# Hybrid decoder trunk on one core: first transfers issued from two queues in another sequence, transfer times in the planner changed, stage order redrawn

## The chip, the core and the metric

The kernel runs on 1 core of one Trainium2 chip. The metric is the device time of one execution in microseconds (us), lower is better: the median of 3 runs. Engines are named as the profile names them: PE (TensorE matmul), PEld (its weight loads), DVE (VectorE), ACT (ScalarE), POOL (GpSimd), SP (SyncE). SPq is the stream of instructions on SP that issues the transfers.

## The reference

Two residual layers over one sequence of 256 positions, width 1024, all float32. Each layer normalises x (RMSNorm), projects it with one wide matrix whose columns belong to several mixers, runs the mixers, multiplies each branch by a SiLU gate and adds the output projection to x.

```python
h = _rmsnorm(x, norm_g[layer])
proj = jnp.einsum('bsd,de->bse', h, w_in)
# layer 0: u_val u_gate z_a q_b k_b v_b z_b, each 512 columns
y_a = _conformer_conv(u_val, u_gate, ...) * silu(z_a)   # 31-tap causal convolution, LayerNorm, SiLU
y_b = moba_attention(q, k, v) * silu(z_b)               # 8 heads of 64
# layer 1: q_c, keys and values, gates, z_c, q_d, k_d, v_d, z_d
y_c = nsa_attention(...) * silu(z_c)   # compressed, selected and window branch
y_d = banded_attention(..., sinks) * silu(z_d)
x = x + jnp.einsum('bse,ed->bsd', concat(y), w_out[layer])
```

## The kernel before

The 256 positions are two token blocks of 128 partitions (`NB` = 2), the width is 8 chunks of 128 (`KC` = 8). A projection of 512 columns is one weight "name" (`ug`, `uv`, `qb`, `kb`, `vb`, `zb`, `za` in layer 0; `kv`, `cc`, `qc`, `kd`, `qd`, `zc`, `zd` in layer 1; `o00` to `o11` for the output projections). `load_w` (L486) loads it in four quarters of 512 KB, each into one of 5 `raw` buffers, and splits each quarter into two parts: `hi` (a cast, ACT or DVE) and `lo` = raw - hi (DVE or POOL). A product then takes three matmuls, hi*hi, hi*lo and lo*hi (`mm3`, L606). Only `ug` is multiplied unsplit, in plain float32, from `raw_ug` and the transposed input `h32`, so that it can begin before any norm is known; the factor of the norm is put in afterwards (`first_block`, L573, with `square_sum`, L560: squares of x, the power -1/2 on POOL, a matmul that spreads the factor `rb`, then `ht` = h32 * rb, its cast `hhi` and the rest `hlo`). The accumulators of projections are two PSUM banks (`pj`), those of attention scores two more (`s`).

In layer 0 the convolution (stages `conv 0` and `conv 1`) is 120 instructions on DVE that add one tap each into `acc_m` or `acc_o`, while PE goes on with qb, kb, vb, zb, za and the attention (`attb` j: scores and softmax of a pair of heads; `pvb` j: the product with the values). `ln`, `ln 2`, `o0` follow, then `norm1 0` and `norm1 1` (the norm of layer 1, one per token block, `norm_block`, L590), which need the output projections of their block: `o0 00` and `o0 01` for block 0, `o0 10` and `o0 11` for block 1.

**What sets the order.** No instruction is issued where it is written. `Recorder` (L172) collects all operations; `issue` (L256) then plays them through a model and emits every engine's instructions in the order that the model gives. Its loop takes for each engine the ready operation with the smallest key and issues the earliest of them (L326):

```python
k = (t, o.seq, 0, 0.0) if e == "SP" else (t, o.rank, o.piece, -o.level)
```

`t` is the modelled start; `rank` is the place of the operation's stage in the list `ORDER` (L404, 128 names), which decides between operations that could start at the same modelled time, that is, whenever an engine has a queue of ready work. Transfers go in program order (`seq`). On the chip each engine runs its instructions in the emitted order, whatever is ready. The costs are in `_cost` (L122): a transfer costs its queue 70 ns (L127). When data land is modelled in L359 to L364: a shared bus from 1400 ns after the issue, 360 bytes per ns, and 900 ns to the end. `free` (L267) says when each engine can begin.

**The first transfers** are all issued by SP in this sequence: `idn` (68 KB: identity and norm weights), `h32` chunk 0, the first half of `ug` quarter 0, chunk 1, the second half, chunks 2 and 3, `ug` quarter 1, x piece 0 and 1 (`X_AT`, L418; together token block 0), `h32` chunks 4 to 7, `ug` quarter 2, x piece 2 and 3 (token block 1), `ug` quarter 3, `prm`, `shp`, then `uv`.

All operations are recorded by one helper, so the profile gives line L384 for nearly all of them; they are told apart by tile names.

## Time and profile before

| | |
|---|---|
| runs | 273.28, 273.89, 274.37 us; median 273.89 |
| profiled execution | 273.76 us, of which its span (first to last instruction) is 271.8 us |
| PE | 262.1 us busy (96% of the span) |
| DVE, ACT, POOL | 195.8, 172.1, 113.8 us busy (72, 63, 42%) |
| granted TensorE clock, mean | 0.994 |
| transfers | 44.89 MB, 165 GB/s in the mean |

The profiled execution has 1.96 us outside its span and stands 0.13 us below the median. Busy PE is modelled: matmuls overlap, so the distance from one start to the next says more than a duration.

### The profile page before, as it was taken

How to read it: one execution, taken by the hardware profiler on the slowest of the kernel's cores; microseconds unless marked ns; L12 is line 12 of the kernel's file. 1: busy time of each engine (PE TensorE's matmuls, PEld its weight loads, DVE VectorE, ACT ScalarE, POOL GpSimd, SP SyncE). 2: the span in 40 equal slices, each digit the busy share in tenths (PEclk: the TensorE clock that was granted, in tenths of full speed). 3: DMA queues.
4: the chain of work that ended last, by engine and by line, in shares of the span. 5: the costliest groups of instructions: out<-in, count | busy, mean ns of one | idle time of the engine just before them, and what ended most of it. 6: DMA issues, size and time to landing. Idle time of an engine off the chain costs nothing.

```text
span 271.8 us, 5006 instructions
## 1 busy us (share of the span) xinstructions
PE 262.1 (96%) x1693; PEld 215.2 (79%) x1693; DVE 195.8 (72%) x510; ACT 172.1 (63%) x457; POOL 113.8 (42%) x145
## 2 busy tenths in 40 slices
PE   7998999999979999999999999999899999999995
PEld 4787987878859989888779888777689977778884
DVE  1379899999998995748977513398999765666241
ACT  2249579799745975836456503598897767886200
POOL 0000079989974504300323746149756042542000
PEclk9999999999979999999999999999999999999999
DMA  6998896655561290521675745699376400000013
GB/s 185 372 407 278 274 329 194 193 165 182 191 219 58 83 295 17 162 67 38 187 247 133 240 140 151 196 393 326 112 239 210 154 4 0 2 1 1 2 39 115
DMA packets 28361, 44.89 MB, mean 165 GB/s; under 512 B 3376, under 2 KB 10288, under 8 KB 28336
## 3 DMA queue, kind: packets, MB, share of 16 engines
q1 hardware_dynamic: 28336, 44.58, 50.3%
q8 instruction: 13, 0.21, 0.3%
q14 instruction: 12, 0.10, 0.1%
HBM read 43.26 MB, written 1.05 MB: 163 GB/s over the span
## 4 chain that ended last, share of the span: by engine, by line
PE 54%; DVE 29%; DMA 8%; issue 3%; SPq 2%; ACT 1%; POOL 0%; DVEq 0%
PE po L384 15%; DVE acc_m L384 8%; DVE acc_o L384 6%; PE pj_za L384 4%; PE pj_zd L384 4%; PE pj_qc L384 4%; PE pj_zc L384 3%; PE pj_zb L384 3%; PE po_c L384 3%; DMA raw_ug<-in_e_w_in_dram 2%; DMA raw_qd<-in_o_w_in_dram 2%; PE pj_cc L384 2%; PE pt_c L384 2%; PE pj_kv L384 2%; DVE ht L384 2%
## 5 line engine op out<-in xcount | busy, mean ns | idle before, releaser
L384 POOL TENSOR_SCALAR p_c<-p_c,r_c 128x128 f32<-128x128 f32 (+1 forms) x32 | 19.4, 621 | 22.8 <-DVE r_c L384 13.9
L384 DVE SCALAR_TENSOR_TENSOR acc_o<-hc,cw,acc_o 128x256 f32<-128x256 f32 x58 | 28.0, 482 | 0.2
L384 DVE SCALAR_TENSOR_TENSOR acc_m<-hc,cw,acc_m 128x256 f32<-128x256 f32 x58 | 27.9, 481 | 0.0
L384 PE MATMUL po<-hi_o,yh 128*128 128x512 f32 (+1 forms) x72 | 26.9, 378 | 0.0
L384 PE MATMUL po<-lo_o,yh 128*128 128x512 f32 (+1 forms) x72 | 26.5, 373 | 0.0
L384 PE MATMUL po<-hi_o,yl 128*128 128x512 f32 (+1 forms) x72 | 26.1, 370 | 0.0
L384 PE MATMUL pj_ug<-h,raw_ug 128*128 128x256 f32 x64 | 17.1, 424 | 1.2 <-DMA raw_ug<-in_e_w_in_dram 1.2
L384 ACT CAST hi_o<-raw_o 128x1024 fp32r<-128x1024 f32 x16 | 16.7, 1055 | 1.9 <-PE pj_zc L384 1.1
L384 DVE TENSOR_TENSOR lo_o<-raw_o,hi_o 128x1024 fp32r<-128x1024 f32 x13 | 15.7, 1221 | 2.5 <-PE pj_zd L384 1.7
L384 POOL TENSOR_TENSOR rsx<-ssx,mhalf 128x1 f32<-128x1 f32 x4 | 2.3, 569 | 34.5 <-DVE ssx L384 34.5
L384 PEld LDWEIGHTS pj_ug<-h,raw_ug 128*128 128x128 f32 x64 | 13.2, 214 | 4.4 <-issue 1.5
L384 ACT ACTIVATE p_c<-sn,mn_c 128x256 f32<-128x256 f32 (+1 forms) x32 | 14.3, 451 | 2.5 <-DVE mn_c L384 2.4
L384 PEld LDWEIGHTS po<-lo_o,yh 128*128 128x128 f32 x72 | 13.5, 188 | 2.5 <-issue 0.5
L384 PEld LDWEIGHTS po<-hi_o,yh 128*128 128x128 f32 x72 | 13.5, 189 | 2.3 <-issue 0.2
L384 PEld LDWEIGHTS po<-hi_o,yl 128*128 128x128 f32 x72 | 13.6, 189 | 2.1
L384 POOL TENSOR_TENSOR lo_kb<-raw_kb,hi_kb 128x1024 fp32r<-128x1024 f32 x3 | 7.3, 2452 | 18.4 <-ACT hi_kb L384 18.4
L384 DVE CUSTOM_DVE_ANT_0 sn<-s_c,shp 128x256 f32<-128x256 f32 (+1 forms) x32 | 10.7, 351 | 3.3 <-ACT p_c L384 3.3
L384 POOL TENSOR_SCALAR p_b<-p_b,r_b 128x128 f32<-128x128 f32 (+1 forms) x16 | 6.7, 436 | 12.6 <-DVE r_b L384 12.6
L384 POOL TENSOR_SCALAR p_d<-p_d,r_d 128x128 f32<-128x128 f32 (+1 forms) x16 | 6.7, 439 | 9.9 <-ACT p_d L384 3.3
L384 ACT ACTIVATE p_b<-sn,mn_b 128x256 f32<-128x256 f32 (+1 forms) x16 | 7.2, 450 | 4.9 <-DVE mn_b L384 4.7
L384 PE MATMUL pj_zc<-hhi,lo_zc 128*128 128x256 f32 x32 | 9.4, 294 | 0.7 <-DVE lo_zc L384 0.7
L384 PE MATMUL pj_zb<-hhi,hi_zb 128*128 128x256 f32 x32 | 9.9, 310 | 0.0
(332 smaller groups left out, 930.1 us busy)
## 6 DMA issues: line engine op xcount, KB each, us to landing
raw_o<-in_w_out_dram SPq DMA_DIRECT2D x16, 512.0 KB, 4.6
raw_uv<-in_e_w_in_dram SPq DMA_DIRECT2D x4, 512.0 KB, 7.7
raw_qb<-in_e_w_in_dram SPq DMA_DIRECT2D x4, 512.0 KB, 4.7
raw_kb<-in_e_w_in_dram SPq DMA_DIRECT2D x4, 512.0 KB, 5.5
raw_vb<-in_e_w_in_dram SPq DMA_DIRECT2D x4, 512.0 KB, 4.4
raw_zb<-in_e_w_in_dram SPq DMA_DIRECT2D x4, 512.0 KB, 3.5
raw_za<-in_e_w_in_dram SPq DMA_DIRECT2D x4, 512.0 KB, 4.2
raw_kv<-in_o_w_in_dram SPq DMA_DIRECT2D x4, 512.0 KB, 3.7
```

The source lines that it names most:

```text
L384: getattr(self.real[e], method)(*args, **kw)
```

## The change

Three things are changed, and no arithmetic.

1. The issue of three transfers (`idn` and the two halves of `ug` quarter 0) goes from SP to the queue of ACT, through `nc.first`: in the model these three cost SP nothing, and ACT is taken to be free from 3200 ns rather than 1880. The sequence of the rest changes: `h32` chunks 4 to 7 now come right after `ug` quarter 1, ahead of `ug` quarter 2, and all four pieces of x come after quarter 2, ahead of quarter 3.
2. The model's transfers: 440 ns on the queue instead of 70; landing begins 1300 ns after the issue, at 300 bytes per ns until 8500 ns and 410 after, and ends 750 ns later.
3. `ORDER` has the same 128 names in another order.

Places of some stages in `ORDER` (0 is the first to be served), before and after:

| stage | before | after | stage | before | after |
|---|---|---|---|---|---|
| conv 0 | 26 | 51 | o0 00 | 25 | 64 |
| conv 1 | 58 | 44 | o0 01 | 24 | 74 |
| attb 0 | 49 | 27 | o0 10 | 45 | 18 |
| attb 1 | 32 | 13 | o0 11 | 123 | 86 |
| attb 2 | 59 | 6 | norm1 0 | 20 | 50 |
| attb 3 | 81 | 114 | norm1 1 | 0 | 5 |
| w zc 0 | 30 | 19 | qd 1 | 14 | 66 |
| w zc 1 | 51 | 36 | qt d | 27 | 9 |
| sc 0 | 5 | 15 | cmp | 63 | 49 |

```diff
--- before.py
+++ after.py
@@ -108,7 +108,7 @@
 class Op:
     def __init__(self, alts, reads, writes):
         self.alts, self.reads, self.writes = alts, reads, writes
-        self.deps, self.succ = set(), []
+        self.deps, self.succ, self.queue = set(), [], None
 
 
 def _views(args, kw):
@@ -124,7 +124,7 @@
     n = w[0].size() if w else 512
     small = min(v.base.psum for v in r) if r else False
     if method == "dma_start":
-        return 70.0
+        return ISSUE_NS
     if engine == "PE":
         if method == "transpose":
             return 109.0
@@ -177,6 +177,7 @@
         self.real = dict(PE=nc.tensor, ACT=nc.scalar, DVE=nc.vector, POOL=nc.gpsimd, SP=nc.sync)
         for e, n in zip(self.ENGINES, ("tensor", "scalar", "vector", "gpsimd", "sync")):
             setattr(self, n, _Front(self, e))
+        self.first = _Front(self, "SP", "ACT")
 
     def stage(self, name):
         self.rank = ORDER.index(name)
@@ -264,7 +265,7 @@
             if o.alts[0][1] == "dma_start":
                 c += 3000
             o.level = c + 130 + max((s.level for s in o.succ), default=0.0)
-        free = dict(PE=600.0, ACT=1880.0, DVE=600.0, POOL=600.0, SP=280.0)
+        free = dict(FREE)
         work = {}
         bus, mode = 0.0, (P, P)
         port = dict(DVE=0.0, POOL=0.0)
@@ -360,8 +361,8 @@
                 o.on = "SP"
                 v = (o.writes or o.reads)[0]
                 bytes_ = 4 * v.size() * (v.box[0][1] - v.box[0][0])
-                bus = max(bus, t + 1400) + bytes_ / 360.0
-                o.end = bus + 900
+                bus = _landing(bus, t, bytes_)
+                o.end = bus + 750
             for b in o.banks:
                 b.last[e] = o.end
             o.done = True
@@ -376,7 +377,7 @@
                 if method == "together":
                     yield from (("PE", *a) for a in args)
                 else:
-                    yield e, method, args, kw
+                    yield o.queue or e, method, args, kw
 
         for e, method, args, kw in parts():
             args = [a.real() if isinstance(a, Ap) else a for a in args]
@@ -385,14 +386,30 @@
 
 
 class _Front:
-    def __init__(self, rec, engine):
-        self.rec, self.engine = rec, engine
+    def __init__(self, rec, engine, queue=None):
+        self.rec, self.engine, self.queue = rec, engine, queue
 
     def __getattr__(self, method):
-        return lambda *args, **kw: self.rec.record((self.engine, method, args, kw))
+        def f(*args, **kw):
+            op = self.rec.record((self.engine, method, args, kw))
+            if self.queue:
+
+                op.queue = self.queue
+                op.alts[0] = (*op.alts[0][:4], 0.0, *op.alts[0][5:])
+            return op
+        return f
+
+
+def _landing(bus, t, nbytes):
+
+    t = max(bus, t + 1300.0)
+    early = min(nbytes, max(0.0, SLOW_UNTIL - t) * 300.0)
+    return t + early / 300.0 + (nbytes - early) / 410.0
 
 
 CYCLE, WINDOW_NS = 5 / 12, 10240 / 3
+FREE = dict(PE=600.0, ACT=3200.0, DVE=600.0, POOL=600.0, SP=280.0)
+ISSUE_NS, SLOW_UNTIL = 440.0, 8500.0
 SWITCH = 95.0
 START = {(64, 128): 120.0, (128, 64): 65.0, (128, 32): 45.0}
 LATENCY = dict(PE=dict(PE=0.0, ACT=200.0, DVE=200.0, POOL=200.0, SP=200.0),
@@ -401,21 +418,20 @@
                POOL=dict(PE=135.0, ACT=100.0, DVE=60.0, POOL=96.0, SP=100.0),
                SP=dict(PE=250.0, ACT=100.0, DVE=100.0, POOL=100.0, SP=100.0))
 EXTRA = dict(copy=(0.0, 20000.0), minus=(80.8, 0.0), scale=(0.0, 20000.0, 20000.0))
-ORDER = ["norm1 1", "attd 2", "w ug 1", "norm0 g0", "pvc 11", "sc 0", "norm0 1", "pvb 3", "kv 1", "w qc 0",
-         "w cc 1", "attc 10", "w o10 1", "zd 2", "qd 1", "w ug 0", "pvd 1", "kd 1", "norm0 r1", "vb 0", "norm1 0",
-         "vb 1", "w qd 0", "zc 3", "o0 01", "o0 00", "conv 0", "qt d", "ln 2", "cc", "w zc 0", "w zb 0", "attb 1",
-         "w o00 0", "o1 10", "norm0 0", "w o01 1", "pvd 0", "pvc 31", "pvb 2", "w qc 1", "ug", "w uv 0", "attc 30",
-         "attc 11", "o0 10", "attd 0", "pvc 00", "attd 1", "attb 0", "zb 0", "w zc 1", "kv 0", "w o10 0", "zb 1",
-         "xc", "qt c", "qc 1", "conv 1", "attb 2", "zb 2", "sc 1", "pvc 21", "cmp", "zd 0", "pvb 0", "zc 0", "kd 0",
-         "pvc 01", "attc 21", "qc 0", "uv", "pvb 1", "zc 1", "qb 0", "zb 3", "qb 1", "zc 2", "o1 00", "pvc 10",
-         "za 0", "attb 3", "pvc 30", "o1 01", "norm0 r0", "w kb 1", "hid", "pvd 2", "w kd 1", "w o01 0", "qd 0",
-         "za 1", "w qb 0", "w kv 0", "w uv 1", "w qb 1", "pvc 20", "w za 1", "attd 3", "w qd 1", "w za 0", "w vb 0",
-         "ln", "w zd 1", "w vb 1", "zd 1", "w kv 1", "w cc 0", "attc 31", "zd 3", "attc 20", "kb 0", "attc 01",
-         "w o11 1", "kb 1", "w o11 0", "pvd 3", "w o00 1", "norm0 g1", "w zd 0", "attc 00", "w zb 1", "o1 11",
-         "o0 11", "za 2", "w kb 0", "za 3", "w kd 0"]
+ORDER = ["norm0 r1", "za 1", "norm0 g1", "w qb 1", "pvb 2", "norm1 1", "attb 2", "zb 1", "kv 1", "qt d", "norm0 1",
+         "attc 01", "norm0 0", "attb 1", "w kb 0", "sc 0", "za 0", "o1 01", "o0 10", "w zc 0", "za 3", "pvb 0",
+         "zd 1", "zc 2", "zc 3", "zb 2", "pvb 1", "attb 0", "uv", "w cc 1", "qb 0", "w o11 0", "w o00 0", "pvc 11",
+         "w kv 1", "za 2", "w zc 1", "zd 2", "w kd 1", "w ug 0", "attc 00", "attd 2", "w uv 1", "pvb 3", "conv 1",
+         "zc 0", "w ug 1", "qb 1", "zb 0", "cmp", "norm1 0", "conv 0", "zb 3", "pvc 01", "hid", "ln 2", "pvd 0",
+         "w o11 1", "w uv 0", "kd 0", "w qb 0", "w qd 1", "pvc 31", "pvc 00", "o0 00", "attc 20", "qd 1", "o1 00",
+         "pvd 1", "pvc 10", "attc 10", "sc 1", "w o10 1", "pvc 21", "o0 01", "w kb 1", "attc 31", "pvd 2", "qc 1",
+         "vb 0", "ug", "w zd 1", "w vb 0", "w zb 1", "w zb 0", "kb 0", "o0 11", "ln", "attc 30", "w za 0",
+         "w o01 1", "kv 0", "vb 1", "xc", "w qc 1", "kd 1", "pvc 20", "qt c", "zd 0", "w za 1", "w qd 0", "cc",
+         "norm0 g0", "w kd 0", "w o01 0", "w cc 0", "attd 1", "w zd 0", "pvd 3", "zd 3", "qc 0", "qd 0", "zc 1",
+         "pvc 30", "attb 3", "attc 21", "o1 10", "w kv 0", "w o10 0", "attd 3", "attc 11", "kb 1", "o1 11",
+         "w qc 0", "w o00 1", "norm0 r0", "w vb 1", "attd 0"]
 RAWS, PARTS = 5, 9
 WARM = 7
-X_AT = ((), (0, 1), (2, 3))
 SUMS_ON_ACT = ('qb', 'kb')
 HEADS_ON_ACT = ("qb", "kb")
 IN_TURN = ("raw", "hi", "lo", "pj", "qn8", "s")
@@ -442,7 +458,7 @@
     idn = const.tile([P, P + KC], F32, name="idn")
     ident, ng = idn[:, :P], idn[:, P:]
     prm = const.tile([P, NPRM], F32, name="prm")
-    nc.sync.dma_start(idn, i["idn"])
+    nc.first.dma_start(idn, i["idn"])
     pieces_x = [(b, slice(q * 512, (q + 1) * 512)) for b in range(NB) for q in range(2)]
 
     def load_x(n):
@@ -499,18 +515,18 @@
             else:
                 raw = raws.tile([P, 2, 512], F32, tag="raw", bufs=RAWS, name=f"raw_{name}{q}")
             o = 0
-            if name == "ug":
-                if q == 0:
-                    nc.sync.dma_start(raw[:, 0], parts[0][0:P, :])
-                    load_xt(1, 1)
-                    nc.sync.dma_start(raw[:, 1], parts[0][P:2 * P, :])
-                    load_xt(2, 2)
-                    quarters.append((raw, None))
-                    continue
-                for n in X_AT[q - 1]:
+            if name == "ug" and q == 0:
+                nc.first.dma_start(raw[:, 0], parts[0][0:P, :])
+                load_xt(1, 1)
+                nc.first.dma_start(raw[:, 1], parts[0][P:2 * P, :])
+                load_xt(2, 2)
+                quarters.append((raw, None))
+                continue
+            if name == "ug" and q == 2:
+                load_xt(4, 4)
+            if name == "ug" and q == 3:
+                for n in range(4):
                     load_x(n)
-                if q == 2:
-                    load_xt(4, 4)
             for p in parts:
                 n = p.shape[1]
                 nc.sync.dma_start(raw[:, :, o:o + n], p[q * 256:q * 256 + 256, :].rearrange("(c p) f -> p c f", p=P))
```

## Rows read from the trace of the kernel before

**Rows 1.** The page: engines' busy time and the chain of waits by engine

```profile
PE 262.1 (96%) x1693; PEld 215.2 (79%) x1693; DVE 195.8 (72%) x510; ACT 172.1 (63%) x457; POOL 113.8 (42%) x145
...
PE 54%; DVE 29%; DMA 8%; issue 3%; SPq 2%; ACT 1%; POOL 0%; DVEq 0%
```

**Rows 2.** Busy time by stretch: stretch, engines (instructions), granted clock, DMA share, GB/s

```profile
35.10:75.70 40.60, 40.57 (x201) 32.72 (x199) 40.56 (x93) 34.87 (x124) 38.22 (x21) 1.00 0.63 204
75.70:85.00 9.30, 7.44 (x47) 6.38 (x45) 8.50 (x35) 5.32 (x20) 3.87 (x3) 0.82 0.51 178
85.00:126.90 41.90, 41.90 (x290) 36.00 (x289) 31.01 (x79) 27.77 (x62) 13.03 (x24) 1.00 0.34 101
```

**Rows 3.** PE's own waits: total us, times, longest

```profile
PE pj_zc L384 <- DVE lo_zc L384: 0.7, 1, 0.7
PE ps_qd_qnorm_g L384 <- DVE qn_qd L384: 0.6, 1, 0.6
```

**Rows 4.** Timeline of PE, first 25 us: start, us, what, wait before

```profile
4.75 4.60 PE L384 MATMUL pj_ug<-h,raw_ug 128*128 128x256 f32 x10 [0.73 <-DMA raw_ug<-in_e_w_in_dram]
9.86 4.25 PE L384 MATMUL pj_ug<-h,raw_ug 128*128 128x256 f32 x18 [0.51 <-DMA raw_ug<-in_e_w_in_dram]
...
23.33 0.39 PE L384 MATMUL pj_uv<-hlo,hi_uv 128*128 128x256 f32 x1 [0.89 <-DVE hlo L384]
```

**Rows 5.** Timeline of SP's queue (issues), then of ACT's first instructions

```profile
3.04 0.43 SPq L384 DMA_DIRECT2D h<-in_prm_dram  x1
3.52 0.43 SPq L384 DMA_DIRECT2D raw_ug<-in_e_w_in_dram  x1
...
0.72 1.28 ACT L384 ACT_TABLE_LOAD   x1 [0.72 <-PEq L1251]
...
8.47 0.51 ACT L384 ACTIVATE h<-h,idn 128x256 f32<-128x256 f32 x1 [6.26 <-DMA h<-in_prm_dram]
```

**Rows 6.** Busy time by stretch, the head (last two columns: DMA share, GB/s)

```profile
2.00:3.00 1.00, 1.00 (x7) 0.57 (x6) 0.00 (x0) 0.20 (x1) 0.00 (x0) 1.00 0.71 128
...
4.75:14.10 9.35, 8.85 (x30) 6.87 (x31) 2.65 (x9) 1.75 (x4) 0.61 (x1) 1.00 0.97 352
```

**Rows 7.** Timeline of all engines: squares of x and norm of the two blocks

```profile
11.03 0.69 DVE L384 CUSTOM_DVE_ANT_0 ht<-x 128x512 f32<-128x512 f32 x1 [2.27 <-DMA x<-in_x_dram]
...
14.66 1.23 DVE L384 TENSOR_TENSOR ht<-h,rb 128x1024 f32<-128x1024 f32 x1 [1.28 <-ACT rb L384]
...
19.12 1.22 DVE L384 TENSOR_TENSOR ht<-h,rb 128x1024 f32<-128x1024 f32 x1
...
22.05 1.22 DVE L384 TENSOR_TENSOR hlo<-ht,hhi 128x1024 fp32r<-128x1024 f32 x1
```

**Rows 8.** Timeline of PE and DVE from 72 to 82 us

```profile
72.10 0.93 PE L384 MATMUL s_b<-qk 64*128 64x128 f32 x8
...
77.65 2.10 PE L384 MATMUL s_b<-qk 64*128 64x128 f32 x8 [1.71 <-DVE mn_b L384]
79.69 0.58 PE L384 MATMUL pj_zb<-hhi,hi_zb 128*128 128x256 f32 x1
...
81.77 0.29 PE L384 MATMUL ps_qk<-idn,qn_qb 128*128 128x128 f32 x1
...
75.75 0.41 DVE L384 CUSTOM_DVE_ANT_0 sn<-s_b,shp 128x256 f32<-128x256 f32 x1
```

**Rows 9.** Timeline of DVE, then of PE and its weight loads, 126 to 134 us

```profile
126.85 0.69 DVE L384 TENSOR_TENSOR x<-x,po 128x512 f32<-128x512 f32 x1
...
132.75 1.27 DVE L384 SCALAR_TENSOR_TENSOR hlo<-ps_ht,hhi 128x512 fp32r<-128x512 f32 x2
...
127.12 0.39 PE L384 MATMUL po<-hi_o,yh 128*128 128x512 f32 x1
...
127.34 0.39 PE L384 MATMUL po<-lo_o,yh 128*128 128x512 f32 x1
...
133.49 0.19 PEld L384 LDWEIGHTS pj_kv<-hi_kv,hlo 128*128 128x128 f32 x1 [0.46 <-DVE hlo L384]
```

## The prediction

> **What bounds the kernel now.** The page first: PE is busy for 262.1 of 271.8 us and holds 54% of the chain that ended last; DVE holds 29% of it [rows 1]. So time can come out only where PE waits or runs slowly, or where DVE keeps PE waiting. The busy time by stretch says where that is: from 35.1 to 75.7 us PE and DVE are both full, from 75.7 to 85.0 PE is busy for 7.44 of 9.30 us at a mean granted clock of 0.82, after that PE is full again while DVE has 10.9 us to spare (31.01 of 41.90) [rows 2]. PE's own longer waits in the middle are three: 1.71 us for the scores of attention [rows 8], and 0.7 and 0.6 us close together near 196 us [rows 3]. The rest is in the head. There the first ten `ug` records in the trace spread over 5.11 us (4.75 to 9.86), where the next eighteen take 4.25, that is 0.24 each; ten should take 2.4, so some 2.7 us are lost to data that were not there, the wait of 0.51 us among them. Later 0.89 us go to a wait for `hlo`, the rest of the second block's norm [rows 4]. Head, score stall and the pair near 196 us are all that a better order can win; the last matmul's result and its way out to memory stay.
>
> **The change, part by part.** All sums are made against the profiled execution, 273.76 us, which is 0.13 below the median of the runs.
>
> *Issue on ACT.* Three issues leave SP. SP's pitch is 0.48 us (3.04 to 3.52) [rows 5], so the transfers behind them go out up to 1.45 us sooner. ACT pays three times 0.43 us before its table load of 1.28 us: its first needed work waits for data until 8.47 us, after an idle 6.26 us [rows 5], so that cover is ample and the cost is nothing. Without that cover it would be 1.3 us.
>
> *Arrival of `ug` quarter 1.* It was issued at 3.52 us, and PE went on with its data at 9.86 [rows 4, 5]. If arrival followed the issue, it would come 1.45 us sooner. If the transfers are bound by bytes, only the idle share can be won: the DMA engines were busy for 0.71 of the third microsecond, so 0.3 us there [rows 6]. I take 0.6, nearer to the lower end, since from 4.75 to 14.10 us the share is 0.97 at 352 GB/s [rows 6]. So `ug`, which PE runs without a wait from 9.86 on, would end some 0.6 us sooner.
>
> *The other sequence.* Now 1.05 MB (`h32` 4 to 7 and `ug` quarter 2) come ahead of x of block 0. At 352 GB/s [rows 6] that is 3.0 us, less the 0.6 to 1.45 by which all starts sooner; I put its square 1.8 us later, at 12.8 instead of 11.03 [rows 7]. From that square to `ht` of block 0 it took 3.6 us (14.66), so `ht` comes at 16.4. Block 1 gains: its x has the same bytes ahead as before, and its squares no longer stand behind the first `ht` on DVE. Its `ht` can follow at 17.7 rather than 19.12 and its `hlo` be done by 20.2 rather than 23.27 (22.05 + 1.22) [rows 7]. PE would then start `uv` when `ug` ends, about 21.7 instead of 23.33: 1.6 us gained. But DVE has its splits of `uv` still to do and starts that run of work (with `ht` of block 0) 1.7 us later, so `uv` can wait for its last `lo`. PE can work on two banks (48 matmuls of 0.12 us, half of 2.08/9 in [rows 8], so 5.6 us) meanwhile. I take half, **-0.8 us**, for the head as a whole; the ends are -3.6 (2.7 and 0.89, all of the lost time) and +1.8 (the delay of block 0's x comes through whole).
>
> *The score stall.* PE issued the scores of the second pair at 77.65 after a wait of 1.71 us, because both banks were held by the first pair, whose scores were out at 73.0 (72.10 + 0.93) and were first read by DVE at 75.75 [rows 8]. Until then DVE did taps of the convolution. After the wait PE ran slowly: the same eight matmuls took 2.10 us, not 0.93, and nine of `pj_zb` took 2.08 (79.69 to 81.77), of which half, 1.0, is the clock's if it ran at half. [...] In the new list `attb` 0, 1 and 2 stand ahead of both halves of the convolution (27, 13, 6 against 44, 51); before, `conv 0` stood ahead of all of them. That speaks for taking all of it, **-3.9**; the ends are -3.9 and 0. What is late next is the convolution: the taps that give way end later, and `ln` behind them; the 10.9 us that DVE has to spare from 85 to 127 [rows 2] hide that.
>
> *The pair near 196 us.* 0.7 us wait for `lo_zc` and 0.6 for `qn_qd` [rows 3]. `w zc` rises (30 and 51 to 19 and 36), but `qd 1` falls (14 to 66). I take half: **-0.6**, between -1.3 and 0.
>
> *The list as a whole.* All 128 places are redrawn, and the present order keeps PE full from 85 to 127 us [rows 2] through many hand-overs between engines. The trace cannot show where the new one waits. I bound it by 0 (the gains of better places are in the terms above, which cover all of PE's longer waits) and by one more stall like the one at 75 us, 3.9; I take two waits like the pair near 196 us, 2 x 1.3 = **+2.6**, the kind that this trace has twice. The model's new transfer times add no instruction: they decide only where in the order things stand, and are costed here.
>
> Sum: -0.8 - 3.9 - 0.6 + 2.6 = -2.7, so 271.1 us from the profiled execution. The runs' median is 0.13 higher: 271.2, and the other times below are put on the median in the same way.
>
> **The rivals.**
>
> *The gains are filled up again (same).* The plan is as wrong as before in other places, or only the earlier issue counts. For it: the score stall comes less from the rank of a stage than from a model that had the scores ready at 75 us when they were ready at 73; `conv 1` stood behind `attb 0` already and its taps were still issued ahead. The head then gives the pitch of one issue at PE's first start, 0.48 us [rows 5], and the stalls change places: 273.9 - 0.5 = 273.4. Against it: the model's transfer times are what was corrected, and the places are moved clearly. [...]
>
> *The norm of layer 1 loses its cover (slower).* From the last add into x of block 0 (126.85) to its `hlo` (134.02) the chain is 7.2 us long, through ACT, POOL, DVE and PE, and PE stood still in it for only 0.46 us, because matmuls of `o0` for the other block were left to do [rows 9]. Each takes 0.22 us (127.12 to 127.34) [rows 9]. In the new list `o0 10` goes first (18), then 00, 01 and 11 (64, 74, 86), and `norm1 0` falls from 20 to 50. If 11 is still whole when block 0 is complete, its 24 matmuls cover 5.3 us and 1.4 more are lost; if it is spent by then, all 6.7 are. With the rest of my sum that is -2.7 + 6.7 = +4.0: 277.9 us. It decides once more than 4.1 us of the chain lie bare. Against it: 11 still stands behind 01.
>
> **How the numbers follow.** A measurement of this kernel can tell about 0.5% from no change, 1.4 us: faster is below 272.5, slower above 275.3. The forecast case, in which at least 1.4 of the 2.7 us come through, has a chance of 0.60 and a range of its own from 266.4 (head and score stall in full, -3.6 and -3.9, the other terms cancelling) to 272.5. The case of no change has 0.21, the bare norm 0.19. The range for 8 in 10 goes from 266.4 to 276.6, which is up to 5.4 of the 6.7 us bare: it leaves out the worst of the slower case and what lies below a head and a stall won whole.
>
> **What would show it.** Head: SP issues `ug` quarter 1 near 2.1 us, ACT's queue three transfers before its table load, PE's second run of `ug` starts near 9.3, and no wait for `hlo` stands ahead of `uv`. Stall: no wait of PE above 1 us from 60 to 100 us, and a granted clock of 1.00 in every stretch of it; scores are read by DVE within 1 us. List: PE's waits after 100 us add up to less than 4 us. I am wrong if PE's waits in total are as long as now, only elsewhere; if `uv` begins after 23.3 because x came late; or if PE stands still ahead of `kv` for microseconds while DVE does the norm.

## The result and the profile after

The changed kernel takes 277.08 us in the median (275.21 to 279.45), the kernel before in the same comparison 272.32 (271.58 to 274.37): a ratio of 1.0149, with a 95% interval from 1.0106 to 1.0193. It is slower by 1.5%, where the forecast was 271.2 us and faster. The profiled execution took 278.38 us with a span of 276.6.

The page of the changed kernel: engines, then the chain that ended last, by engine.

```profile
PE 265.9 (96%) x1693; PEld 216.1 (78%) x1693; DVE 192.2 (69%) x511; ACT 171.5 (62%) x457; POOL 109.2 (39%) x144
...
PE 64%; DVE 18%; DMA 11%; issue 2%; SPq 1%; POOL 1%; ACT 1%; ACTq 0%; DVEq 0%
```

Against [rows 1] PE's share of the chain rose from 54 to 64% and DVE's fell from 29 to 18: DVE binds less, and still the span grew by 4.8 us. PE is busy 3.8 us longer at equal work, so part of the loss stands as slow or drawn-out matmuls, not as idle time.

Busy time of the changed kernel by stretch (columns as in [rows 2]):

```profile
24.00:26.00 2.00, 0.20 (x1) 0.23 (x2) 2.00 (x5) 2.00 (x4) 1.75 (x1) 0.98 0.28 57
26.00:28.00 2.00, 2.00 (x11) 2.00 (x11) 2.00 (x3) 2.00 (x6) 1.56 (x1) 0.50 0.57 213
28.00:30.00 2.00, 2.00 (x14) 2.00 (x14) 2.00 (x3) 1.19 (x2) 0.00 (x0) 0.67 0.55 164
35.10:75.70 40.60, 39.81 (x208) 32.50 (x207) 39.42 (x94) 34.20 (x124) 32.95 (x19) 1.00 0.63 202
75.70:85.00 9.30, 8.90 (x59) 6.95 (x58) 9.30 (x40) 8.39 (x24) 6.92 (x11) 1.00 0.61 202
85.00:126.90 41.90, 41.90 (x293) 36.29 (x292) 34.97 (x80) 29.99 (x65) 11.03 (x17) 1.00 0.39 122
```

The score stall of [rows 2] is nearly gone: 8.90 of 9.30 us busy at a full clock, where it was 7.44 at 0.82. A new hole has opened in the head: from 24 to 26 us PE does next to nothing while DVE and ACT are full, and then runs two microseconds at a granted clock of 0.50 and two at 0.67 in the mean. That slow part alone is 1.7 us (2 x 0.50 + 2 x 0.33).

Timeline of the changed kernel's head, PE and then ACT and DVE; it answers to [rows 4] and [rows 7]:

```profile
4.87 2.05 PE L385 MATMUL pj_ug<-h,raw_ug 128*128 128x256 f32 x4 [0.86 <-DMA raw_ug<-in_e_w_in_dram]
7.85 2.47 PE L385 MATMUL pj_ug<-h,raw_ug 128*128 128x256 f32 x5 [0.93 <-DMA raw_ug<-in_e_w_in_dram]
...
18.31 0.39 PE L385 MATMUL ps_r<-dg,ones 128*128 128x128 f32 x2
...
25.80 0.44 PE L385 MATMUL pj_uv<-hhi,hi_uv 128*128 128x256 f32 x1 [2.13 <-DVE sg L385]
...
12.27 0.63 ACT L385 ACTIVATE ht<-x 128x512 f32<-128x512 f32 x1 [1.56 <-DMA x<-in_x_dram]
...
18.73 0.27 ACT L385 COPY rb<-ps_r 128x128 f32<-128x128 f32 x1 [4.38 <-PE ps_r L385]
...
14.91 0.28 DVE L385 TENSOR_SCALAR dg<-idn,rsx 128x128 f32<-128x128 f32 x1
...
19.02 2.36 DVE L385 TENSOR_TENSOR ht<-h,rb 128x1024 f32<-128x1024 f32 x2 [2.34 <-ACT rb L385]
...
24.10 1.22 DVE L385 TENSOR_TENSOR hlo<-ht,hhi 128x1024 fp32r<-128x1024 f32 x1
```

x came as forecast: its square is at 12.27 and 12.97 us (ACT and DVE), 12.8 was said. `dg`, the diagonal that carries the norm of block 0, is ready at 15.19. But PE multiplies it by `ones` (`ps_r`) only at 18.31 (13.94 before): the emitted order of PE has 21 matmuls of `ug` ahead of it, 14 before the change (the trace has two records for each), and those run late, since the second half of `ug`'s first quarter was not there until 7.7 us. ACT waits 4.38 us for `ps_r`, DVE 2.34 for ACT, and PE at last 2.13 for DVE: one lateness, handed round three engines. `uv` ends 3.6 us later than before (38.91 against 35.28).

PE also runs the first of these matmuls at half its later pace. Two pieces of its timeline, and the 38 records up to `ps_r` as the chain of waits has them:

```profile
9.69 1.91 PE L385 MATMUL pj_ug<-h,raw_ug 128*128 128x256 f32 x4
13.78 1.46 PE L385 MATMUL pj_ug<-h,raw_ug 128*128 128x256 f32 x6
...
7.85 10.62 PE pj_ug L385 x38
```

Records start 0.43 us apart up to 12.3 us and 0.22 apart from there on; before the change the same step lies at 10.1 us. In each trace the record of the granted clock begins only at that step, so the 1.00 that the rows by stretch print for the time ahead of it ([rows 6] too) was not measured. Where it does show 0.50, from 25.9 to 29.3 us, the records of `pj_uv` start 0.21 us apart (27.54, 27.75, 27.97), and behind that, at 1.00, 0.12 apart (29.65, 29.76, 29.88). That the clock was low at the start as well is an estimate from these two changes of pace. In the second profiles of the two kernels the record begins at 13.7 us (changed) and 3.7 us (before). At the 0.24 us a record of [rows 4], 38 would have taken 9.0 us and not 10.62.

The transfers of the first 9 us (KB each, median us from issue to landing), changed kernel:

```profile
raw_ug<-in_e_w_in_dram SPq DMA_DIRECT2D x3, 512.0 KB, 7.7
...
raw_ug<-in_e_w_in_dram ACTq DMA_DIRECT2D x2, 256.0 KB, 4.8
```

and the kernel before:

```profile
raw_ug<-in_e_w_in_dram SPq DMA_DIRECT2D x3, 512.0 KB, 7.9
...
raw_ug<-in_e_w_in_dram SPq DMA_DIRECT2D x2, 256.0 KB, 3.3
```

The two pieces that PE wants first go out sooner from ACT and land later after their issue, 4.8 against 3.3 us. The first is there at 4.7 us (4.6 before), so its earlier issue wins nothing; the second takes 6.07 us and is there at 7.7 (6.3 before), together with the piece of `h32` that SP issues at the same time (1.64 us, landed at 7.6) and that SP issued behind it before the change.

What follows the head, by the end of two stages in both traces: at the end of `kb` the change is 3.7 us behind (61.76 against 58.08), at the end of `cc` 2.5 (153.92 against 151.46), at the last matmul 4.7 (273.27 against 268.54). So between the end of `uv` and that of `cc` the change wins 1.1 to 1.2 us back, and it loses 2.3 behind `cc`; both are put down to the new list here. In the second profiles of the two kernels it is 5.2 us behind at the end of `uv`, 3.3 at the end of `cc` and 4.9 at the last matmul: 1.9 won and 1.6 lost. The loss begins here (PE, POOL and SP of the changed kernel, then pieces of its chain of waits):

```profile
161.45 1.02 PE L385 MATMUL ps_hid<-w1k,xc 128*32 128x256 f32 x4 [0.30 <-POOL xc L385]
...
159.19 3.41 POOL L385 TENSOR_TENSOR xc<-sw,prm 64x120 f32<-64x120 f32 x8 [2.81 <-DMA sw<-kv]
...
155.36 1.16 SPq L385 DMA_DIRECT2D sw<-kv  x2
...
155.36 3.77 DMA sw<-kv
165.81 4.95 DMA w1v<-in_c_v_w_dram
171.48 6.21 DMA raw_qd<-in_o_w_in_dram
178.41 4.41 DMA raw_zc<-in_o_w_in_dram
```

`hid` now stands 2.4 us sooner than before (161.45 against 163.86), though the work before it is 2.5 us late. PE meets it while GpSimd is still adding up `xc`, and in the chain of waits the transfers of `w1v`, `qd` and `zc` follow one another behind it.

### The profile page after: what moved, and what is told of

The parts are those of the page before. It is cut to its first block, busy times and chain, and to the rows that moved or that the text cites. A ratio compares the mean times of both kernels' runs of the same rounds, so it can differ in the third digit from the quotient of the medians.

```text
span 276.6 us, 5006 instructions
## 1 busy us (share of the span) xinstructions
PE 265.9 (96%) x1693; PEld 216.1 (78%) x1693; DVE 192.2 (69%) x511; ACT 171.5 (62%) x457; POOL 109.2 (39%) x144
## 4 chain that ended last, share of the span: by engine, by line
PE 64%; DVE 18%; DMA 11%; issue 2%; SPq 1%; POOL 1%; ACT 1%; ACTq 0%; DVEq 0%
PE po L385 16%; DVE acc_o L385 6%; DVE acc_m L385 6%; PE pj_zd L385 4%; PE pj_zc L385 4%; PE pj_kv L385 4%; PE pj_za L385 4%; PE pj_ug L385 4%; PE pj_zb L385 3%; PE po_c L385 3%; PE pj_uv L385 2%; DMA raw_qd<-in_o_w_in_dram 2%; DMA raw_ug<-in_e_w_in_dram 2%; PE pt_c L385 2%; DMA raw_kb<-in_e_w_in_dram 2%
## 5 line engine op out<-in xcount | busy, mean ns | idle before, releaser
L385 POOL TENSOR_SCALAR p_c<-p_c,r_c 128x128 f32<-128x128 f32 (+1 forms) x32 | 18.1, 583 | 19.9 <-PE s_c L385 8.1
L385 DVE TENSOR_TENSOR lo_o<-raw_o,hi_o 128x1024 fp32r<-128x1024 f32 x15 | 18.2, 1221 | 2.8 <-ACT hi_o L385 2.7
L385 PE MATMUL pj_ug<-h,raw_ug 128*128 128x256 f32 x64 | 17.7, 439 | 1.8 <-DMA raw_ug<-in_e_w_in_dram 1.8
L385 PEld LDWEIGHTS pj_ug<-h,raw_ug 128*128 128x128 f32 x64 | 13.9, 223 | 5.2 <-issue 1.6
L385 POOL TENSOR_TENSOR rsx<-ssx,mhalf 128x1 f32<-128x1 f32 x4 | 3.2, 788 | 36.5 <-DVE ssx L385 36.5
L385 ACT CAST hi_o<-raw_o 128x1024 fp32r<-128x1024 f32 x16 | 16.4, 1050 | 0.1
L385 DVE TENSOR_TENSOR x<-x,po 128x512 f32<-128x512 f32 (+1 forms) x9 | 5.7, 628 | 9.5 <-PE po L385 9.5
L385 POOL TENSOR_SCALAR p_d<-p_d,r_d 128x128 f32<-128x128 f32 (+1 forms) x16 | 6.7, 435 | 14.0 <-DVE r_d L385 11.3
L385 DVE TENSOR_REDUCE ss_qc<-sq_qc 128x8 f32<-128x512 f32 x2 | 1.4, 686 | 15.2 <-ACT sq_qc L385 15.2
L385 PE MATMUL pj_uv<-hhi,hi_uv 128*128 128x256 f32 x32 | 9.8, 307 | 2.1 <-DVE sg L385 2.1
L385 ACT ACTIVATE sq_qc<-pj_qc 128x512 f32<-128x512 f32 x2 | 1.2, 597 | 15.0 <-PE pj_qc L385 15.0
L385 POOL TENSOR_TENSOR lo_za<-raw_za,hi_za 128x1024 fp32r<-128x1024 f32 x4 | 9.5, 2392 | 2.2 <-ACT hi_za L385 2.2
```

Of the source, the lines that this page charges most:

```text
L385: getattr(self.real[e], method)(*args, **kw)
```

## Experiments

Theory A: the head loses the time, because the first pieces of `ug` come late and `ps_r` has a fixed place behind matmuls of `ug`. Theory B: the new list loses it. Theory C: x's later place in the sequence loses it. Ratios are to the kernel before, with 95% intervals; A is when `uv`'s last matmul ends, B the rest of the span, both of the profiled execution.

```
kernel               ratio                    A      B
before, two profiles 1                        35.3   236.5;  34.7  236.9
changed, two         1.0149 (1.0106, 1.0193)  38.9   237.7;  39.9  236.7
a1_sp                1.0101 (1.0063, 1.0140)  35.7   238.6
a2_spread_early      1.0074 (1.0052, 1.0097)  35.9   238.0
b1_sp_spread_early   1.0113 (1.0043, 1.0184)  35.4   237.6
d1_before_act        1.0033 (0.9986, 1.0079)  36.3   237.4
e3_x_sooner          1.0208 (1.0142, 1.0274)  39.8   237.7
f1_head_of_before    1.0244 (1.0211, 1.0277)  39.6   237.9
f2_head_xc_qn        1.0172 (1.0131, 1.0213)  39.2   236.8
a3_old_list          1.0709 (1.0625, 1.0794)  39.0   251.3
c1_hid_later         1.0217 (1.0145, 1.0290)  39.2   238.5
c2_sp_early_hid      1.0170 (1.0103, 1.0237)  36.3   237.8
e1_xc_sooner         1.0108 (1.0029, 1.0188)  39.1   236.3
e2_head_xc_qn, three 1.0102 (1.0063, 1.0141)  35.4   236.2;  38.3  236.9;  37.8  236.9
a4_before_scores_fi. 1.0039 (0.9999, 1.0078)  34.9   236.2
h1_taps_later        1.0070 (1.0040, 1.0099)  35.5   239.6
```

**The queue.** In the changed kernel the three first transfers go back to SP; in the kernel before they go to ACT.

```diff
# a1_sp, in issue() of the changed kernel
-                    yield o.queue or e, method, args, kw
+                    yield e, method, args, kw
# d1_before_act, in issue() of the kernel before
+        loads = [o for o, alt in order if alt[1] == "dma_start"]
+        named = lambda n: [o for o in loads if o.writes and o.writes[0].base.name.startswith(n)]
+        first = named("idn")[:1] + named("raw_ug0")[:2]
...
-                    yield e, method, args, kw
+                    yield "ACT" if o in first else e, method, args, kw
```

> The changed kernel, with the three first transfers (identity and the two halves of ug's first quarter) issued by SP, ahead of h, and nothing else moved: the order of PE, DVE and GpSimd stays as the plan wrote it. If the split over two queues delays ug's first quarter (theory A), its second half lands by about 6 us rather than 7.7, PE's second run of ug matmuls starts near 6.5 rather than 7.85 us, the reduction ps_r of block 0 comes 1 to 1.8 us before 18.3, and the time falls from 277 to about 275.3. If the loss sits in the new list downstream (B) or in x's later place in the sequence of transfers (C), uv starts at 25.8 us as before and the time stays at 277.

> The kernel before with one part of the change alone: identity and the two halves of ug's first quarter are issued by ACT in place of SP; plan, order and every other transfer stay. By theory A the second half of ug's first quarter shares the 16 DMA engines with h and later pieces of ug and lands later after its issue (near 6 us instead of 3.3), PE's second run of ug matmuls and with it ps_r come 0.5 to 2 us later than 13.9, and the time rises by 0.5 to 2 us. By the prediction's head term the first pieces land sooner, and the time falls by about 0.6 us.

The landing time goes with the queue, in either kernel (the same view, a1_sp and then d1_before_act):

```profile
raw_ug<-in_e_w_in_dram SPq DMA_DIRECT2D x2, 256.0 KB, 3.1
```

```profile
raw_ug<-in_e_w_in_dram ACTq DMA_DIRECT2D x2, 256.0 KB, 4.8
```

With SP, `ps_r` runs at 16.65 rather than 18.31 and `uv` starts at 24.14 rather than 25.80, as A said. Although PE waits the same 2.13 us for `sg`, the clock does not fall behind that wait this time (0.998 in the mean of the profile, 0.994 in the changed kernel's), and `uv` ends at 35.7. So in these profiles 1.7 of the 4.4 us by which `ps_r` came late go with the queue, the pace included (0.43 us a record until 10.3 us here); 2.7 stay. The ratio of 1.0101 is 275.1 us on the 272.32 of the first comparison, near the 275.3 expected, but its interval overlaps that of the changed kernel. With ACT in the kernel before, PE waits 2.79 us for `ug` and runs at a clock of 0.50 from 7.9 to 11.3 us; `ps_r` and `uv`'s end come 1.1 and 1.0 us later (15.04 and 36.3). That profiled execution was the slowest of its ten (275.48 us, median 274.71). The time rises by 0.3%, which its interval can't tell from none. So the queue's cost in the head is shown by the landing times and the traces of both kernels; by time it is not shown in either.

**PE's place for `ps_r`.** Block 0's goes behind 14 matmuls of `ug`, block 1's behind 17.

```diff
# a2_spread_early, in issue() of the changed kernel
+        ug = [p for p in order if named(p[0], "pj_ug")]
...
+        late = ug[14:n1]
+        order = [p for p in order if p not in late]
+        at = order.index(r0) + 1
+        order[at:at] = late[:3]
+        at = order.index(r1) + 1
+        order[at:at] = late[3:]
```

> The changed kernel, with the two reductions ps_r of the first norm put earlier in PE's written order: block 0's behind 14 matmuls of ug in place of 21, block 1's behind 17 in place of 23; the matmuls they pass follow them. By theory A (the norm's reductions are stuck behind ug matmuls that run late, and uv and the slow clock follow from that) ps_r of block 0 runs at about 15.3 us, uv starts near 23.5 rather than 25.8, the slow clock at 26 to 29 us goes, and the time falls by 2 to 3.7 us to about 274. By B (list downstream) it stays at 277. By C (x late) the reduction can't run before the diagonal matmuls, some 15.2 us, and gains at most what lies between that and 18.3, so C agrees with A here, but leaves uv no earlier than 23.

> The changed kernel with both repairs of the head: the three first transfers issued by SP, and the reductions ps_r earlier in PE's order. Theory A': each of the two repairs brought uv's end back to within 0.6 us of the kernel before (35.7 and 35.9 against 35.3 us, where the change had 38.9), because both cure the same lateness, so together they add little: uv ends at 35.2 to 35.8 us and the time is that of the better one, ratio to before 1.005 to 1.008; what is left over before is then the list's. Rival: the two cures are of different delays and add up, then uv ends near 33 us and the ratio is 0.998 or less.

`ps_r` runs at 16.17, later than expected: the second piece of `ug` still comes from ACT's queue, and the clock was at 0.50 from 7.0 to 13.9 us. `uv` starts at 24.20 and ends at 35.9, and half of the loss is gone by time (1.0074 is 274.3 us on 272.32, with an interval clear of the changed kernel's). b1, a1 and a2 together, ends `uv` hardly sooner (35.4), as expected; its ratio is above the forecast 1.005 to 1.008, and its interval covers those of both. That the two cure the same lateness is one reading. The other is a floor: in b1 PE waits 1.7 us for `dg`, which hangs on x, so `ps_r` could not run much before 15.5 whatever stood ahead of it.

**The place of x.** In the changed kernel, x's first block goes back ahead of the last four chunks of h.

```diff
# e3_x_sooner, in issue() of the changed kernel
+        x0 = [p for p in loads if named(p, "x0")]
+        h = [p for p in loads if named(p, "h32")]
+        order = [p for p in order if p not in x0]
+        at = order.index(h[3])
+        order[at:at] = x0
```

> The changed kernel with the two pieces of x's first block back at their place in the sequence of the kernel before, ahead of the last four chunks of h; nothing else moves. By theory C (x late makes the norm late) the square of block 0 is about 1 us sooner than 12.3, uv starts near 24 us rather than 25.8 and the time falls by 1 to 2 us. By theory A the reduction ps_r stands behind 21 matmuls of ug, which now wait longer for h: the square is sooner, ps_r is not (18.3 us or later), uv starts at 25.8 or later, and the time is 277 to 278.5.

C's gain does not come, and A's forecast was too mild: `ps_r` comes at 19.20 and `uv` at 26.70. But the edit can't clear x either: not even the square is sooner (12.56 on ACT), because ACT and DVE have the scaling of h ahead of it in their own order and now wait for h:

```profile
12.15 0.51 ACT L392 ACTIVATE h<-h,idn 128x256 f32<-128x256 f32 x1 [3.38 <-DMA h<-in_prm_dram]
12.56 0.61 ACT L392 ACTIVATE ht<-x 128x512 f32<-128x512 f32 x1
```

**The whole head of before.** Queue, place of x and place of block 0's `ps_r` together, with the plan's other orders as changed. f2 adds the edits xc and qn of a later part.

```diff
# f1_head_of_before: a1_sp, e3_x_sooner, and in issue()
+        late = [u for u in ug[14:] if order.index(u) < order.index(r0)]
...
+        order[at:at] = late
```

> The changed kernel with the whole head of the kernel before: all first transfers on SP, x's first block ahead of the last chunks of h, and ps_r of block 0 behind 14 matmuls of ug; list, plan and everything behind the head stay as changed. The edits so far cured one part each: with ps_r early but x late, PE waited 2.6 to 2.8 us for the diagonal dg, and the clock was at 0.5 between 15 and 22 us in two of three profiles. If queue, place of x and place of ps_r are one loss together, uv starts at 21 to 22 us and ends by 35.5 with a full clock, and what is left over before is the list alone: by the traces +1 to +1.5 us, so a ratio of 1.003 to 1.006 where the change had 1.015. If the head is not the larger part, the ratio stays above 1.009.

> The same with hid's input sooner (two transfers sw, four additions of xc on DVE) and the copy qn_kb ahead of the cast. By trace the first is worth about 1.4 us behind 150 us, the second up to 0.9 near 60 us. If they add to the head's repair, the time is 0.8 to 2 us below f1's and level with the kernel before or below it: ratio 0.996 to 1.001. If not, it is f1's.

Neither gain comes: `uv` ends at 39.6 and 39.2. The waits of PE and ACT in f1 say why:

```profile
15.35 0.49 PE L399 MATMUL ps_r<-dg,ones 128*128 128x128 f32 x2 [1.52 <-DVE dg L399]
...
21.25 0.39 PE L399 MATMUL ps_r<-dg,ones 128*128 128x128 f32 x2
...
27.61 0.36 PE L399 MATMUL pj_uv<-hhi,hi_uv 128*128 128x256 f32 x1 [2.09 <-ACT hi_uv L399]
...
21.67 0.27 ACT L399 COPY rb<-ps_r 128x128 f32<-128x128 f32 x1 [5.53 <-PE ps_r L399]
21.83 1.05 ACT L399 CAST hhi<-ht 128x1024 fp32r<-128x1024 f32 x1
```

DVE and ACT scale the late h ahead of x's squares; and ACT's order has the copy for block 1 ahead of `hhi` of block 0, so block 0's operand, ready to be split at 17.9 us (16.70 + 1.22), waits 4 us more for block 1's `ps_r`. The kernel before splits block 0 at 15.92 already. The head's orders on four engines were made for one timetable of transfers; put back a part of the old timetable, and the rest stands wrong.

**The list.** The changed kernel gets the ORDER of the kernel before, planned with the new transfer times.

```diff
-ORDER = ["norm0 r1", "za 1", "norm0 g1", "w qb 1", "pvb 2", "norm1 1", "attb 2", "zb 1", "kv 1", "qt d", "norm0 1",
+ORDER = ["norm1 1", "attd 2", "w ug 1", "norm0 g0", "pvc 11", "sc 0", "norm0 1", "pvb 3", "kv 1", "w qc 0",
...
```

> The changed kernel with the list of stages of the kernel before; transfers, queues and the transfer times of the plan stay as changed, and the plan is made again. By B (the new list costs the time) it comes back to 272.3 or below. By A and C (the head costs it) it stays at 276 or above, and by the trace the stall of 85 us (score matmul behind the convolution taps on DVE) is there again, which would make it 279 to 281.

292.31 us, far beyond either expectation: 1.071 of before. `uv` ends at 39.0, so the head is as late as in the changed kernel, and the rest is 13.6 us longer; PE waits 4.3 us for `qn_kn` and 2.6 for `mn_c`, waits that are 0.2 and 0.3 us or less in the other two. So this list does badly with transfer times other than those that it was found with, and this run can't tell the list's share. The counterpart, the new list with the old transfers and their times, was not run. What the list costs is read from column B instead.

**`hid`.** First its groups go later on PE: 8 matmuls of `qc` are pulled ahead of the first, the rest of block 0's ahead of the third, 14 of `kd` ahead of the fourth (c1; c2 has a1 and a2 as well). Then, with PE's order kept, its input comes sooner (e1; e2 has a1, a2 and qn as well).

```diff
# c1_hid_later, in issue() of the changed kernel
+        for group, name, n in ((hid[0], "pj_qc0", 8), (hid[2], "pj_qc0", 20), (hid[3], "pj_kd0", 14)):
+            at = order.index(group)
+            pull = [p for p in order[at:] if named(p, name) and p[1][0] == "PE"][:n]
...
# xc: e1_xc_sooner
+        at = order.index(kv) + 1
+        order[at:at] = sw
+        adds = [p for p in order if named(p, "xc_") and p[1][1] == "tensor_tensor"][-8:]
+        for p in adds[::2]:
+            order[order.index(p)] = (p[0], ("DVE", *p[1][1:]))
# qn: in e2 and f2
+        qn = next(p for p in act if named(p, "qn_kb") and p[1][1] == "copy")
...
+        order.insert(order.index(qn) + 1, ahead)
```

> The changed kernel with the four groups of ps_hid put later in PE's written order: 8 matmuls of pj_qc are pulled ahead of the first group, the rest of block 0's pj_qc ahead of the third, 14 of pj_kd ahead of the fourth; nothing else moves. If the list's loss at 160 to 172 us is PE waiting in its fixed order for GpSimd's xc and for w1v (the first two groups took 3.1 us after a wait, against 1.9 in the kernel before), those groups fall to about 1.9 us each pair, PE loses about 1 us instead of 4.7 in 160 to 170 us, and the time falls by 1.5 to 3 us, to about 274.5. If that loss is covered anyway (qd's transfers, issued behind w1's, set the pace), kd or qd wait instead and the time stays at 277.

> The changed kernel with all three edits: first transfers on SP, ps_r early, groups of ps_hid later. If head and hid are the two losses and are independent, the gains add: 2 to 2.7 for the head and 1.5 to 3 for hid, 277 falls to 271.5 to 273.5, level with the kernel before or below it (ratio 0.993 to 1.001). If an earlier head only lets PE wait longer later (DVE's convolution, the transfers of qd), the gain is that of the larger edit alone, ratio near 1.005.

> The changed kernel with the input of hid made sooner and PE's order kept: the two transfers sw are issued right behind the copy of kv that they read (they stood behind one transfer of w1), and four of the eight last additions that make xc run on DVE in place of GpSimd. If the chain from sw by xc to hid, and from there by the freed buffers to w1, qd and zc, is what the new list loses at 155 to 190 us, hid starts 1 to 1.8 us sooner than 161.45, the chain's later transfers move with it, and the time falls by 1 to 2 us, to 275 to 276. If the chain is not what binds, hid starts sooner and the time stays at 277.

> The changed kernel with four edits: first transfers on SP, ps_r early, hid's input sooner, and on ACT the copy qn_kb ahead of the cast hi_zb that stood before it (PE waits 0.8 us for that copy near 61 us). If head, hid and this wait are separate losses, the gains add: 2 to 2.7 for the head, 1 to 2 for hid, 0.5 to 0.9 for the copy, so 3.5 to 5.5 off 277: 271.5 to 273.5, a ratio to the kernel before of 0.99 to 0.999. If they only trade with one another, the ratio stays at 1.007 or above.

Later groups win nothing. The ratios are 0.7 points above the changed kernel (c1) and 0.6 above b1 (c2), with intervals that overlap; by trace the last matmul comes 1.1 to 1.2 us later in both (274.42 against 273.27, 270.84 against 269.67). That is the rival's case: `qd` starts at 179.27 us where it started at 179.25, and PE now waits for what `hid` and `qc` give (its own waits from 160 to 200 us, c1; total, times, longest):

```profile
PE ps_kcv L393 <- DVE hx L393: 0.8, 1, 0.8
PE ps_qc_qnorm_g L393 <- DVE qn_qc L393: 0.5, 1, 0.5
PE ps_hidT L393 <- ACT hid L393: 0.5, 1, 0.5
PE ps_kd L393 <- ACT qTn L393: 0.4, 1, 0.4
```

With a sooner `xc` (e1) `hid` starts at 160.68 rather than 161.45 and B is 236.3, and B lies between 236.2 and 236.9 in every kernel with that edit. The changed kernel has 237.7 in one profile but 236.7 in the other, without the edit, so a gain of 1 us is not shown. By time e1 falls by 0.4 points, to 275.3 us on 272.32, but its interval reaches well into that of the changed kernel. So `hid`'s wait is real, but what it is worth stays open. The gains of e2 don't add up as hoped either: 1.0102 where 0.99 to 0.999 was expected. e2's profile had no slow stretch (a granted clock of 0.999 in the mean) and a span of 271.7, that of the kernel before; but its runs' median was 275.95, so it was profiled again.

**The same kernel again.**

> The kernel of the four edits (head_xc_qn), unchanged, profiled a second time. Its first profile had a full clock throughout and a span of 271.7, but the median of its runs was 2.3 us above the profiled one. If the missing 2.3 us are a fall of the clock in some executions, this profile shows 0.5 over 2 to 6 us, most likely at 8 to 14 us where PE has waited for ug, or near 60 to 80, and a span near 274. If they sit in a wait instead, the clock is full and one stage of PE is 2 us longer than in the first profile.

> The same kernel a third time, to tell a rule from an accident: as for the second profile.

> The kernel before, unchanged, profiled a second time. If the clock's fall belongs to the kernel (it falls where PE has just waited), the granted clock is 0.5 again within 77 to 84 us and nowhere else, uv ends at 35 to 36 us, and the span is 271 to 273. If the fall is a matter of the run, the second profile has it in another place or not at all, and spans of 269 to 274 are possible.

> The changed kernel, unchanged, profiled a second time. If the fall of the clock after PE's wait for uv is the kernel's own, it is at 26 to 30 us again and uv ends near 38.9. If not, uv ends 1.5 to 2 us sooner and the span is that much shorter, 274 to 275.

Busy time by stretch, second profile of e2's kernel (columns as in [rows 2]):

```profile
12.00:14.00 2.00, 0.67 (x4) 0.24 (x2) 0.72 (x3) 0.88 (x3) 0.00 (x0) 1.00 1.05 393
14.00:16.00 2.00, 0.53 (x2) 0.53 (x3) 1.11 (x5) 0.57 (x2) 1.00 (x2) 0.69 1.05 406
16.00:18.00 2.00, 2.00 (x7) 1.64 (x6) 1.76 (x6) 0.27 (x1) 0.13 (x1) 0.50 1.05 407
18.00:20.00 2.00, 2.00 (x7) 1.64 (x7) 0.42 (x2) 0.70 (x2) 0.00 (x0) 0.50 1.05 408
20.00:22.00 2.00, 2.00 (x7) 1.63 (x6) 2.00 (x6) 2.00 (x3) 0.00 (x0) 0.61 1.05 409
```

Where PE waits for `dg` in e2's first and second profile:

```profile
15.61 0.49 PE L411 MATMUL ps_r<-dg,ones 128*128 128x128 f32 x2 [2.62 <-DVE dg L411]
15.47 0.80 PE L411 MATMUL ps_r<-dg,ones 128*128 128x128 f32 x2 [2.80 <-DVE dg L411]
```

Most of the time that these two profiles lose against the first goes to the clock, in the head: a granted clock of 0.50 for 6.8 us (3.4 us lost, of a span 3.5 us longer), and for 3.4 us in the third profile (1.7 lost of 3.0), in or right behind a wait of `ps_r` for `dg` of 2.80 and 2.57 us. The first profile had the same wait (2.62) and no fall. That wait is x: `ps_r` stands early now and x comes late, so C holds in this one sense. In the kernel before the clock fell at 78 to 82 us in both profiles (to 0.50 in the first), behind its score stall; in the changed kernel at 26 to 31 in both.

The clock does not explain why this kernel stays behind the kernel before. Every run has a mean granted clock on record: the four of e2's twelve at 0.997 or more took 274.8 us in the mean, the other eight 276.5; of the 17 runs of the kernel before in the same comparison, the eight at 1.000 took 272.1 and the other nine 274.3. Like against like, 2.2 to 2.7 us are left, and three of the four took 275.0 to 275.4, so the first profile's 273.62 owes something to more than that clock; the clock at the start, which these means leave out, may be part of it and was not measured.

**The score stall.** In the kernel before, DVE's convolution taps go later: seven, and those in between, behind the first four maxima (a4); then the whole remaining stretch by ten places (h1).

```diff
# a4_before_scores_first, in issue() of the kernel before
+        late = [p for p in conv if order.index(p) < first][-7:] + [p for p in conv if first < order.index(p) < last]
...
+        order[at:at] = late
# h1_taps_later, in issue() of the kernel before
+        taps = taps[ahead - 7:]
+        moved = dict(zip(map(id, taps[10:]), taps))
+        last = taps[-1]
+        order = [q for p in order for q in ([moved.get(id(p))] if id(p) in moved else [] if p in taps else [p]) +
+                 (taps[-10:] if p is last else [])]
```

> The kernel before with one edit of DVE's written order: the convolution taps that stood ahead of and between the first four negated-maximum instructions of attention block 0 are moved behind these four. This is the prediction's score term alone. If the score stall was worth what its row said, PE loses about 1.3 us rather than 4.2 in 75 to 85 us, the clock there stays up, and the time falls by 2.9 to 3.9 us, to about 268.5 to 269.4. If another wait takes its place (the convolution comes later, and who reads it), the time stays near 272.3.

> The kernel before with DVE's convolution taps from the seventh ahead of attention block 0's first negated maximum on put ten places later among DVE's work, so that the maxima of block 0, the product z and the maxima of block 1 all come sooner; the taps' result is read at 100.65 us and they end near 95 now, so ten taps of 0.39 us fit. The earlier edit moved seven taps behind block 0's maxima alone, and PE then waited 2.1 us for z in place of 1.7 for the maximum. If the prediction's price of the score stall (2.9 to 3.9 us) is right when the whole stretch is moved, PE's wait and the clock's fall at 77 to 82 us go, PE loses about 1 us rather than 4.8 between 70 and 90 us, and the ratio to the kernel before is 0.986 to 0.992. If DVE's work is the bound of that stretch in whatever order, the wait turns up again at the next reader (maxima of blocks 2 and 3, ps_y at 100 us) and the ratio is 0.997 to 1.003.

a4 wins nothing by time: PE gets the second scores at 75.23, 2.4 us sooner, and then waits 2.13 us for `z`, which stands behind the moved taps, with the clock at 0.50 from 82 to 84. h1 wins it all at first: PE is full from 66 to 95 us, and the scores of the third group and the end of `zb` come 3.5 us sooner than before. Then it pays (PE's waits from 66 to 110 us, and the first `ps_y`):

```profile
PE ps_y L393 <- DVE y_b L393: 3.6, 2, 3.3
...
100.60 0.33 PE L393 MATMUL ps_y<-idn,ya 128*128 128x128 f32 x1 [3.28 <-DVE y_b L393]
```

Ten taps in a row on DVE (91.50 to 96.7) hold up `y_b`, the clock falls there too (0.93 from 100 to 102 us, 0.50 to 104, 0.72 to 106), and the last matmul is 3.3 us later. So the stall's price of 2.9 to 3.9 us was right where it stood, and in both of these edits moving DVE's taps was paid for elsewhere. That a thinner spread of them, as the new list has it, escapes this is not shown apart from the rest of the list.

No kernel tried beats the kernel before.

## Why the prediction was wrong

**The step that failed is the head, and in it the arrival of data at PE's fixed order.** It was taken at -0.8 with ends of -3.6 and +1.8; it measured +3.6 in one profile (38.9 against 35.3) and +5.2 in the other (39.9 against 34.7). Four things in it:

- *"That cover is ample and the cost is nothing"* looked at ACT's time alone. The transfers themselves paid: 4.8 us from issue to landing in place of 3.3. The rival in which only the earlier issue counts, 0.48 us at PE's first start, had half of it. That little was to be won by an earlier issue agrees with the trace: the DMA share is 1.02 at 381 GB/s from 4.87 to 14.10 us, and PE's first start came no sooner (4.87, 4.75 before). That a second queue changes nothing else does not agree: it also changed which bytes came first, and the second piece of `ug` came 1.5 us later than before. What the forecast took for quarter 1, 0.6 us sooner, was about right (landed at 8.9 us, 9.7 before), but PE was still at quarter 0.
- *"So `ht` comes at 16.4"* carried over the 3.6 us from square to `ht` of [rows 7]. The square was right (12.8 said, 12.3 and 13.0 measured), the rest wasn't: `ht` came at 19.02, because between them stands `ps_r`, an instruction of PE, and the new plan had put 21 matmuls ahead of it. The chain over the engines was 6.75 us long (12.27 to 19.02): its length did not outlast the new neighbours of one link.
- The start of `uv` at *"about 21.7"* fell with it, and the wait of 2.13 us that took its place was followed by a slow clock that cost 1.7 us more (a1 had the same wait without the fall). The forecast had named this sign ("if `uv` begins after 23.3 because x came late") and given it a bound of 1.8, without the clock.
- *"Ten should take 2.4"* put all of 2.7 us down to missing data. Part of it is PE's pace: the records start 0.43 us apart until 10.1 us. Before the change that cost little, since quarter 1 landed only at 9.7 us; in the changed kernel, with a late second piece and 21 matmuls ahead of `ps_r`, the slow pace up to 12.3 us counts. The forecast has no term for it.

By time, a2 shows the head's share: half of the loss goes with PE's place for `ps_r` alone. How the rest of it divides between the queue and the clock at the start is read from single traces.

**The score stall**, -3.9 (1.7 of wait, 1.2 for the scores and 1.0 for `pj_zb`): right in size (h1 wins 3.5 us there). The slow part is shown: the granted clock of the kernel before was 0.50 from 78.4 to 81.8 us, the eight scores took 2.10 us in place of 0.93, and the records of `pj_zb` start 0.21 us apart in place of 0.12. And the list took most of the stall itself (the wait went from 1.71 to 0.40 us, the clock to 1.00). But its other end was named wrongly. That the 10.9 us which DVE has to spare hide the late convolution holds for the sum of DVE's time and not for its order: up to the end of `cc` 1.2 us are left of the 3.9 (1.9 in the other pair of profiles), a new wait of PE's for `qn_kb` (0.8 us at 61) among what took the rest.

**The list's new waits and the pair**, +2.6 and -0.6: together +2.0 forecast, +2.3 measured behind `cc` in one pair of profiles and +1.6 in the other. The size came out by luck, since it was guessed; the places are `hid`'s `xc`, then `keep` for `qd` (0.9 us at 181).

**The rivals.** The bare norm did not come: PE is busy for 19.98 us from 125 to 145. The slow side was right, by another mechanism. Head and list together are +3.6 - 1.2 + 2.3 = 4.7 of the 4.8 us by trace, 4.1 by the ratio. The sum was also set on a base of three runs, 273.89 us; the eleven runs of the comparison have 272.32, so the miss is larger than the times say: -2.7 forecast, +4.1 measured.

**What stays open:** what the clock costs at the start, where no record of it stands and only the pace of the matmuls speaks; what the list costs alone, which no run tells apart; and whether a plan made for the transfers as they are, from one queue, with this list's spread of the taps would win, which was not run.

## What to carry to other kernels

Where a planner writes fixed orders for several engines, its model of the first transfers, its list and its order are one piece: test a change of one only with the others planned and measured again. A part put back may bring back a part of the time (a2, half) or lose more (f1, 1.0 point). When a chain over engines is forecast, count for each link what stands ahead of it in that engine's own order after the change. And a stall has an owner: if a full engine made it, ask first where its work would go; in both edits here moving the work moved the stall (to 2.13 us for `z` in a4, 3.28 for `y_b` in h1).

## What was not expected

The clock made one kernel into two. The same binary, e2's, had a full clock in the head in one execution and 0.50 for 6.8 us in another, with a wait of 2.62 us in the first and 2.80 in the second; spans were 271.7 and 275.2. In its three profiles the clock's record begins at 4.7, 4.5 and 10.2 us, and the fall comes not at all, at 14.8 and at 17.0; why they differ is not shown. A single profile of such a kernel is one draw: e2's first was the luckiest of twelve runs (273.62 us, with a median of 275.95).
